# A hybrid attention, gMLP and gated-MLP layer on one core: w_down loaded by quarters, the start of the gate and down stages reordered, part of a norm and of four operand sums on other engines

## The chip, the cores and the metric

The kernel runs on one core of a Trainium2 chip. The metric is the device time of one execution in microseconds (us), the median of several runs. The core has five engines: TensorE (PE in the profile, with PEld for its weight loads), VectorE (DVE), ScalarE (ACT), GpSimd (POOL) and SyncE (SP), whose queue issues nearly all transfers here.

## What is computed

One layer on 1024 tokens of width 1024, cut to what matters here. The first two lines make `x1`; g and up are the gate stage, f the down stage.

```python
mix = concat(diff_attention(...), spatial_gating(...)) @ w_out      # 1024 x 1024
x1  = layer_norm(ALPHA * x + mix, ln1_g, ln1_b)
g   = causal_dwconv(x1 @ w_gate, conv_w, conv_b)                    # 1024 x 2816, width 3
up  = x1 @ w_up                                                     # 1024 x 2816
f   = (silu(g) * up) @ w_down                                       # 2816 x 1024
out = layer_norm(ALPHA * x1 + f, ln2_g, ln2_b)
```

All is float32. Each operand of a large product is split into a high part and a low part (`split`, L214: ScalarE rounds the high part, VectorE or another engine subtracts it from the source for the low part), and `mm3` (L218) makes three matmuls of it: high x high (L220), high x low (L221), low x high (L222).

## The kernel before

The kernel goes through stages: input projections and gMLP, attention (an order written by a list scheduler, L673 to L863), output projection with the first norm (L1061 to L1089), the gate stage (gate and up products with convolution and Silu, up to L1142), the down stage (L1146 to L1254) with the second norm. Outside the attention the tile framework orders the instructions: the program order is the priority, and by an internal estimate of times it moves instructions that are ready ahead of ones that are not, on each engine and on SP's queue too. What runs on an engine or a queue is then a fixed order, and each instruction waits in it for its inputs and for its tile to be free. Pools with `reuse_waits="tile"` may take the place of a released pool and wait only for the tiles that they cover.

**Products of quarters.** Gate, up and down products use a scheme of seven products for a 2 x 2 block product (P1 to P7) in place of eight. `QA` (L904) names the left operand of each (quarters A11, A12, A22 and sums S1 to S4), `QB` (L905) the right one (quarters B11, B21, B22 and sums T1 to T4). In the gate stage the A's are quarters of x1 transposed; a unit u is a pair of 128-column blocks of w_gate (u even) or w_up (u odd), 22 units in all, and one product of a unit is 12 matmuls. In the down stage the A's are quarters and sums of silu(g) * up, which the gate stage writes to DRAM (`yd`, L1045) and the down stage reads back (`ya`); the B's are quarters of w_down, 256 rows to a step m, eleven steps for each product name, in the order P1, P2, P6, P5, P7, P4, P3. A down step is 12 matmuls too (four token tiles by three, `d_mm`).

**From the output projection to the gate stage.** In the loop over t (L1075) each token tile gets its second half, then `lnorm` (L879): statistics, a power on GpSimd, and for each half one subtract-and-scale (L886) and one scale-and-add (L891) on VectorE; with `spread` the latter becomes a scaling on ScalarE (L888) and an addition on GpSimd (L889). `x1_transp(t)` (L914) transposes a tile on TensorE (L925); ScalarE copies and VectorE splits the result, and for tiles 4 to 7 VectorE adds A21 + A22 = S1 (L929). Then `x1_sums` (L936) makes S1's split, S2 = S1 - A11, S3 = A11 - A21 and S4 = A12 - S2, on VectorE (L944), each with a split. In program order come: the transposes of all tiles, S1, two prepared weights, S2, two more, S3, S4 (L1125 to L1135), then the products in the order `seq` (L1097): P1 and P2 of units 0 and 1, then (0, P5), (0, P6), (1, P5), (0, P7), (1, P6), (0, P4), (0, P3), (1, P7). `prepare(n)` (L1118) loads gate weights and makes the first n entries of `order` (T1 of unit 0 first).

**From the gate stage to the down stage.** All 22 blocks of 128 rows of w_down are loaded one after the other (L1148 to L1153), 512 KB each, ten into a new pool `wdp` over the places of the released pools `fp` (gate results) and `qp` (raw gate weights), twelve into tiles `kslot`, which the gate stage uses for prepared weights and S3, S4. Then `d_prep(name, m)` (L1158), kept `DAHEAD` = 4 steps ahead of `d_mm`, loads `ya` and splits both operands; for P6 it also makes T2 by three subtractions on VectorE (L1168 to L1171). Tiles `xslot` (20) hold x1's quarters, S1 and S2 in the gate stage and `ya` and the splits in the down stage.

## Time and profile before

| | |
|---|---|
| time, median of 3 runs | 1119.82 us (1119.18 to 1121.28) |
| profiled execution, its own time | 1121.76 us |
| span of the profiled execution | 1120.1 us |
| PE busy, matmuls | 1069.4 us (95%), 4974 |
| DVE busy | 811.1 us (72%) |
| ACT busy | 476.6 us (43%) |
| POOL busy | 180.7 us (16%) |
| mean granted TensorE clock | 0.982 of full speed |
| DMA | 109.61 MB, 98 GB/s in the mean |

The profile is of one execution. A busy share of an engine says nothing of what waits: that is read from the list of waits, from the timeline of an engine, and from stage tables, which give for a stretch of time (from the span's start) the busy time of each engine and the clock that TensorE was granted, as a share of 2.4 GHz; 0.50 is its lower level, 1.2 GHz. A line number is one of the kernel before; a helper's line (L215, L216 for `split`; L220 to L222 for `mm3`) stands for all of its uses, which the names of the tiles tell apart: `wT`, `wB` are prepared gate weights, `do` and `yo` the split operands of the down stage, `wd` the loaded w_down, `fA` the transposed quarters and their sums, `ps` a PSUM bank.

### The profile page before, as it was taken

Reading aid. Unit: us, or ns where it says so; the run is one execution under the profiler, and the core shown is the slowest. Engines: PE = TensorE matmul, PEld = TensorE weight load, DVE = VectorE, ACT = ScalarE, POOL = GpSimd, SP = SyncE. Lnnn points to the kernel's source line nnn. Section 1 sums busy time; section 2 is a strip of 40 time slices with the busy share of each in tenths; the row PEclk is TensorE's granted clock in tenths of the full one; section 3 lists DMA queues with packets and bytes.
Section 4 is the critical chain, followed back from the end, with each engine's and each line's share of the span. In section 5 each row is a group of like instructions: output and inputs, shape, how many; then the busy total and the mean of one; then the engine's idle time right before and its main releaser. Section 6 shows DMA issues by size and latency. Waiting matters only on the chain.

```text
span 1120.1 us, 13859 instructions
## 1 busy us (share of the span) xinstructions
PE 1069.4 (95%) x4974; PEld 877.7 (78%) x4974; DVE 811.1 (72%) x1349; ACT 476.6 (43%) x894; POOL 180.7 (16%) x209
## 2 busy tenths in 40 slices
PE   9999999888999999899999999999999489999996
PEld 6888887667788887688888888888887368888885
DVE  5337257789998669997677767776876379854777
ACT  5511113348677313565344434443443154444342
POOL 2014044476544011000000000000000000000036
PEclk9999999989999999899999999999999799999999
DMA  7400202111200511032332333133314953423333
GB/s 256 145 10 10 94 27 68 38 38 44 71 11 29 176 49 40 16 132 98 113 123 69 112 112 129 58 113 123 121 39 156 341 198 106 139 87 102 100 98 123
DMA packets 50053, 109.61 MB, mean 98 GB/s; under 512 B 5760, under 2 KB 6288, under 8 KB 49984
## 3 DMA queue, kind: packets, MB, share of 16 engines
q1 hardware_dynamic: 48944, 105.40, 27.8%
q0 software_dynamic: 1040, 3.32, 1.0%
q8 instruction: 39, 0.64, 0.2%
q14 instruction: 30, 0.25, 0.1%
HBM read 82.23 MB, written 24.38 MB: 95 GB/s over the span
## 4 chain that ended last, share of the span: by engine, by line
PE 76%; DVE 13%; DMA 3%; ACT 3%; issue 2%; POOL 2%; SPq 1%; DVEq 0%; POOLq 0%; ACTq 0%
PE ps L222 23%; PE ps L221 23%; PE ps L220 23%; DVE t L438 2%; PE ps L617 2%; DVE p L586 1%; POOL t L441 1%; DVE qs L470 1%; DVE x L886 1%; DMA ya<-yd 1%; PE ps L603 1%; DMA wd<-w_down 1%; PE ps L540 1%; POOL uT L362 1%; DMA zraw<-w_vz 1%
## 5 line engine op out<-in xcount | busy, mean ns | idle before, releaser
L220 PE MATMUL ps<-do,yo 128*128 128x512 f32 x308 | 122.0, 396 | 16.1 <-ACT do L215 16.1
L221 PE MATMUL ps<-do,yo 128*128 128x512 f32 x308 | 122.2, 397 | 0.8 <-DVE do L216 0.8
L222 PE MATMUL ps<-do,yo 128*128 128x512 f32 x308 | 121.5, 394 | 0.0
L216 DVE TENSOR_TENSOR wT<-wq,wT 128x512 fp32r<-128x512 f32 x88 | 60.3, 688 | 34.6 <-ACT wT L215 34.5
L1241 POOL DMA_DIRECT2D g<-ln_g x1 | 0.6, 577 | 520.5 <-DVE do L216 520.5
L216 DVE TENSOR_TENSOR yo<-ya,yo 128x512 fp32r<-128x512 f32 x77 | 54.4, 706 | 39.1 <-ACT yo L215 39.1
L220 PEld LDWEIGHTS ps<-do,yo 128*128 128x128 f32 x308 | 58.9, 191 | 29.8 <-ACT do L215 17.0
L215 ACT ACTIVATE yo<-ya 128x512 fp32r<-128x512 f32 x77 | 48.2, 625 | 76.8 <-DMA ya<-yd 53.7
L215 ACT ACTIVATE wT<-wq 128x512 fp32r<-128x512 f32 x88 | 55.3, 632 | 52.1 <-PE ps L222 46.4
L221 PEld LDWEIGHTS ps<-do,yo 128*128 128x128 f32 x308 | 58.8, 191 | 14.7 <-DVE do L216 2.4
L222 PEld LDWEIGHTS ps<-do,yo 128*128 128x128 f32 x308 | 58.9, 191 | 12.1
L216 DVE TENSOR_TENSOR wB<-wq,wB 128x512 fp32r<-128x512 f32 x66 | 45.5, 690 | 26.8 <-ACT wB L215 24.6
L215 ACT ACTIVATE wB<-wq 128x512 fp32r<-128x512 f32 x66 | 41.3, 631 | 50.2 <-PE ps L222 35.3
L966 DVE TENSOR_TENSOR wq<-wq,wq 128x512 f32<-128x512 f32 x88 | 60.6, 691 | 2.6
L1032 DVE SCALAR_TENSOR_TENSOR c<-g,cw,c 128x1023 f32<-128x1023 f32 (+1 forms) x44 | 56.3, 1279 | 8.0 <-ACT c L1030 7.9
L216 DVE TENSOR_TENSOR do<-wd,do 128x512 fp32r<-128x512 f32 x66 | 45.2, 685 | 19.7 <-ACT do L215 19.7
L215 ACT ACTIVATE do<-wd 128x512 fp32r<-128x512 f32 x66 | 41.0, 621 | 38.2 <-DMA wd<-w_down 19.1
L222 PE MATMUL ps<-xh,qw 128*128 128x512 f32 x128 | 50.9, 398 | 4.2 <-DVE qw L216 4.2
L220 PE MATMUL ps<-xh,qw 128*128 128x512 f32 x128 | 50.9, 397 | 2.2 <-ACT qw L215 2.2
L565 ACT ACTIVATE p<-ps,mx 128x384 f32<-128x384 f32 (+7 forms) x64 | 47.3, 744 | 8.3 <-DVE mx L555 4.4
L221 PE MATMUL ps<-xl,qw 128*128 128x512 f32 x128 | 50.5, 394 | 0.0
L220 PE MATMUL ps<-zw,xh 128*128 128x512 f32 x128 | 49.8, 389 | 0.0
(241 smaller groups left out, 2958.2 us busy)
## 6 DMA issues: line engine op xcount, KB each, us to landing
ya<-yd SPq DMA_DIRECT2D x77, 256.0 KB, 2.9
wq<-w_gate SPq DMA_DIRECT2D x44, 256.0 KB, 2.8
wq<-w_up SPq DMA_DIRECT2D x44, 256.0 KB, 2.8
yd<-u SPq DMA_DIRECT2D x22, 512.0 KB, 3.1
wd<-w_down SPq DMA_DIRECT2D x22, 512.0 KB, 7.3
zraw<-w_vz SPq DMA_DIRECT2D x23, 256.0 KB, 3.1
yd<-c SPq DMA_DIRECT2D x11, 512.0 KB, 2.7
qraw<-w_qk SPq DMA_DIRECT2D x8, 512.0 KB, 3.6
```

Of the source, the lines that this page charges most:

```text
L215: A.activation(hi, src, AF.Copy)
L216: (lo_eng or V).tensor_tensor(lo, src, hi.bitcast(F32), op=ALU.subtract)
L220: PE.matmul(po, lhsT=lh, rhs=rh, start=start, stop=False, skip_group_check=onto)
L221: PE.matmul(po, lhsT=lh, rhs=rl, start=False, stop=False, skip_group_check=onto)
L222: PE.matmul(po, lhsT=ll, rhs=rh, start=False, stop=stop, skip_group_check=onto)
L362: GP.tensor_tensor(u, u, gt.rearrange("p c t -> p (c t)"), op=ALU.mult)
L438: eng.tensor_tensor(t[2][o], pt[i], sin_s[i, cols], op=ALU.mult)
L441: GP.tensor_tensor(t[1], t[1], t[2], op=ALU.add)
L565: A.activation(p[:, 0:L].rearrange("p (b n) -> p b n", b=nb), sc, AF.Exp, bias=st_mx[n][:, j : j + 1], accum_out=sm[:, j : j + 1],)
L617: PE.matmul(st_o[h, i][:, j * DV : (j + 1) * DV], lhsT=st_at[h, i][kt // 4][:, kt % 4, j], rhs=vr[kt // 2][:, kt % 2, h * DV : (h + 1) * D ...
L966: sub = lambda o, a, b: V.tensor_tensor(q[o], q[a], q[b], op=ALU.subtract)
L1032: V.scalar_tensor_tensor(t[:, n:S], g[:, 0 : S - n], cw[:, f, 2 - n : 3 - n], t[:, n:S], op0=ALU.mult, op1=ALU.add)
```

## The change

It does five things.

1. **w_down by quarters.** Each 128 x 1024 block becomes two loads of 128 x 512, issued by `d_loads` just ahead of the product that first needs the quarter: B11 for P1, B21 and B12 for P2, B22 for P6, with `ya` of the same step. Loads run `LAHEAD` = 3 steps ahead of the splits. B11 and B21 of steps 0 to 3 go to tiles of `qp`, which now stays open; the others of steps 0 to 4 to `wdp`, now only over the place of `fp`; the rest to `kslot`.
2. **First down steps in the gate stage.** The loads and splits of P1's steps 0, 1 and 2 are placed behind P2, P6 and P4 of the last unit.
3. **First gate products earlier.** The transposes of tiles 6 and 7 and the sums S1 to S4 are no longer ahead of all products: they follow the first four (`fill_in`). T3 of unit 0 is prepared before S4.
4. **S3 and S4 on GpSimd.** A11 - A21 is taken on GpSimd tile by tile right behind S1's addition, in place; S4's two subtractions go to GpSimd.
5. **The last tile's first norm spread.** For t = 7 `lnorm` uses ScalarE and GpSimd for the second half of its work.

```diff
@@ -31,6 +31,7 @@
 NEG = -1.0e30
 AHEAD = 4
 DAHEAD = 4
+LAHEAD = 3
 SPAN = []
 SCB = 3
 WARM = 10
@@ -926,7 +927,9 @@
             for n in range(2):
                 src = pt[:, 2 * n : 2 * n + 2, :]
                 if name == "A22":
-                    V.tensor_tensor(xf["S1"][n][:, :, tk], xf["A21"][n][:, :, tk], src, op=ALU.add)
+                    f = xf["A21"][n][:, :, tk]
+                    V.tensor_tensor(xf["S1"][n][:, :, tk], f, src, op=ALU.add)
+                    GP.tensor_tensor(f, xf["A11"][n][:, :, tk], f, op=ALU.subtract)
                 else:
                     A.copy(xf[name][n][:, :, tk], src)
                 if name != "A21":
@@ -934,14 +937,13 @@
                     split(hi[:, :, tk], lo[:, :, tk], src)
 
     def x1_sums(name):
-        a, b, slot = {
-            "S1": (None, None, xslot), "S2": ("S1", "A11", xslot), "S3": ("A11", "A21", kslot), "S4": ("A12", "S1", kslot)
-        }[name]
         o = {"S1": "S1", "S2": "S1", "S3": "A21", "S4": "A12"}[name]
-        x_operand(name, slot)
+        x_operand(name, xslot if name in ("S1", "S2") else kslot)
         for n in range(2):
-            if a:
-                V.tensor_tensor(xf[o][n], xf[a][n], xf[b][n], op=ALU.subtract)
+            if name == "S2":
+                V.tensor_tensor(xf[o][n], xf["S1"][n], xf["A11"][n], op=ALU.subtract)
+            elif name == "S4":
+                GP.tensor_tensor(xf[o][n], xf["A12"][n], xf["S1"][n], op=ALU.subtract)
             split(*xo[name][n], xf[o][n])
 
     raws_w, opw, acc_w, dst_w = {}, {}, {}, {}
@@ -1079,7 +1081,7 @@
             e = (n + H) % (2 * H)
             mm_out(pt, t, e, 1, n == 0, n == 2 * H - 1)
         fill_x(t, pt, 1)
-        lnorm(op, x1[t], stats[t], x1[t], g1, b1)
+        lnorm(op, x1[t], stats[t], x1[t], g1, b1, None, t < NT - 1)
         if 2 <= t < 6:
             x1_transp(t - 2)
         if t == 5:
@@ -1122,46 +1124,42 @@
             w_prep(u, name)
             done[0] += 1
 
-    x1_transp(6)
-    x1_transp(7)
-    release(op)
-    fp = tc.alloc_tile_pool(name="fp", bufs=1, reuse_waits="tile")
-    dram = tc.alloc_tile_pool(name="dram", bufs=1, space=bass.MemoryType.DRAM)
-    x1_sums("S1")
-    prepare(2)
-    x1_sums("S2")
-    prepare(4)
-    x1_sums("S3")
-    x1_sums("S4")
-
-
-    for i, (u, name) in enumerate(seq):
-        prepare(max(0, i + AHEAD - 4))
-        product(u, name)
-        outputs(u, name)
-    release(fp)
-    release(qp)
-
-
-    wdp = tc.alloc_tile_pool(name="wdp", bufs=1, reuse_waits="tile")
-    wq = {}
-    for m in range(NM):
-        for kh in range(2):
-            t = wdp.tile([P, D], F32, name=nm("wd")) if m < 5 else kslot([P, D], "wd", F32)
-            f = 2 * m + kh
-            nc.sync.dma_start(t, w_down[f * P : (f + 1) * P, :])
-            wq[m, f"B{kh + 1}1"], wq[m, f"B{kh + 1}2"] = t[:, LEFT], t[:, RIGHT]
-    rows = {}
-    down_seq = [(n, m) for n in ("P1", "P2", "P6", "P5", "P7", "P4", "P3") for m in range(NM)]
+
+    rows, wq, where, wdp = {}, {}, {}, []
+    DORDER = ("P1", "P2", "P6", "P5", "P7", "P4", "P3")
+    down_seq = [(n, m) for n in DORDER for m in range(NM)]
     ya, dop = {}, {}
+    loaded = [0]
+
+    def quarter(m, b):
+
+        if m < 4 and b in ("B11", "B21"):
+            return tslot("dq")
+        if m < 5:
+            return wdp[0].tile([P, 512], F32, name=nm("dq"))
+        key = m, b[1]
+        if key not in where:
+            where[key] = kslot([P, D], "dq", F32)
+        return where[key][:, LEFT if b[2] == "1" else RIGHT]
+
+    def d_load(name, m):
+        a = QA[name]
+        if m % 2 == 0:
+            ya[a, m // 2] = xslot([P, 2, 512], "ya", F32)
+            for i in range(min(2, NM - m)):
+                nc.sync.dma_start(ya[a, m // 2][:, i, :], yd[m + i][:, YI[a], :])
+        for b in {"P1": ("B11",), "P2": ("B21", "B12"), "P6": ("B22",)}.get(name, ()):
+            t = wq[m, b] = quarter(m, b)
+            f, c = 2 * m + int(b[1]) - 1, LEFT if b[2] == "1" else RIGHT
+            nc.sync.dma_start(t, w_down[f * P : (f + 1) * P, c])
+
+    def d_loads(upto):
+        while loaded[0] < min(upto, len(down_seq)) and (wdp or down_seq[loaded[0]][1] < 4):
+            d_load(*down_seq[loaded[0]])
+            loaded[0] += 1
 
     def d_prep(name, m):
         a, b = QA[name], QB[name]
-        if m % 2 == 0:
-            n = min(2, NM - m)
-            ya[a] = xslot([P, 2, 512], "ya", F32)
-            for i in range(n):
-                nc.sync.dma_start(ya[a][:, i, :], yd[m + i][:, YI[a], :])
         sub = lambda o, x_, y_: V.tensor_tensor(o, x_, y_, op=ALU.subtract)
         src = {"T1": "B11", "T3": "B12", "T4": "B21"}.get(b, b)
         if b == "T2":
@@ -1172,16 +1170,41 @@
         elif b == "T3":
             sub(wq[m, "B12"], wq[m, "B22"], wq[m, "B12"])
         ta, tb = xslot([P, 2, 512], "yo"), xslot([P, 2, 512], "do")
-        split(ta[:, 0], ta[:, 1], ya[a][:, m % 2, :])
+        split(ta[:, 0], ta[:, 1], ya[a, m // 2][:, m % 2, :])
         split(tb[:, 0], tb[:, 1], wq[m, src])
         dop[name, m] = ta, tb
 
     ready = [0]
 
     def d_prepare(upto):
+        d_loads(upto + LAHEAD)
         while ready[0] < min(upto, len(down_seq)):
             d_prep(*down_seq[ready[0]])
             ready[0] += 1
+
+    release(op)
+    fp = tc.alloc_tile_pool(name="fp", bufs=1, reuse_waits="tile")
+    dram = tc.alloc_tile_pool(name="dram", bufs=1, space=bass.MemoryType.DRAM)
+    fill_in = [
+        lambda: x1_transp(6), lambda: x1_transp(7), lambda: (x1_sums("S1"), prepare(1)),
+        lambda: (x1_sums("S2"), prepare(4), x1_sums("S3"), prepare(5), x1_sums("S4")),
+    ]
+
+
+    for i, (u, name) in enumerate(seq):
+        prepare(max(0, i + AHEAD - 4))
+        product(u, name)
+        outputs(u, name)
+        if i < len(fill_in):
+            fill_in[i]()
+        if (u, name) == (NU - 1, "P2"):
+            d_prepare(1)
+        if (u, name) == (NU - 1, "P6"):
+            d_prepare(2)
+        if (u, name) == (NU - 1, "P4"):
+            d_prepare(3)
+    release(fp)
+    wdp.append(tc.alloc_tile_pool(name="wdp", bufs=1, reuse_waits="tile"))
 
     dacc = {}
 
@@ -1229,9 +1252,9 @@
         def store(c):
             nc.sync.dma_start(out[t * P : (t + 1) * P, c], r[:, c])
 
-        lnorm(wdp, r, stats2[t], r, rows["g2"], rows["b2"], store, spread)
-
+        lnorm(wdp[0], r, stats2[t], r, rows["g2"], rows["b2"], store, spread)
...
         if name in ("P1", "P2", "P5"):
             for j in range(4):
                 dacc[j, DK.get(name, "a")] = ps1()
@@ -1252,7 +1275,8 @@
                 for m in range(whole, NM):
                     d_mm(name, m, j)
                 d_out(name, j)
-    release(wdp)
+    release(wdp[0])
+    release(qp)
     release(stk)
     for p in reversed(psum):
         p.release()
```

## Rows read from the trace of the kernel before

**Rows 1.** Stage table: from:to, length, busy per engine (instructions), clock, DMA share, GB/s.

```profile
441.00:478.00 37.00, 30.39 (x131) 24.30 (x130) 35.81 (x56) 19.06 (x36) 0.92 (x1) 0.86 0.09 29
478.00:867.00 389.00, 389.00 (x1718) 322.09 (x1717) 292.74 (x412) 173.87 (x259) 0.00 (x0) 1.00 0.30 106
867.00:908.00 41.00, 22.16 (x72) 16.07 (x72) 17.25 (x28) 9.49 (x17) 0.00 (x0) 0.75 0.90 337
908.00:1072.00 164.00, 163.98 (x724) 135.44 (x723) 121.77 (x197) 73.69 (x129) 1.11 (x2) 1.00 0.33 105
```

**Rows 2.** Waits of TensorE, whole run: who <- for whom: us, times, longest.

```profile
PE ps L220 <- ACT do L215: 16.1, 2, 12.7
PE ps L220 <- ACT wT L215: 4.3, 1, 4.3
...
PE ps L925 <- DVE x L891: 2.1, 1, 2.1
PE ps L220 <- ACT u L1007: 1.7, 1, 1.7
...
PE ps L220 <- ACT u L1009: 0.7, 1, 0.7
```

**Rows 3.** Stage table for four stretches right behind waits of TensorE.

```profile
446.60:450.60 4.00, 3.99 (x14) 3.28 (x15) 3.71 (x11) 2.91 (x9) 0.00 (x0) 0.57 0.00 0
472.90:477.80 4.90, 4.78 (x10) 3.30 (x11) 4.84 (x8) 1.58 (x4) 0.00 (x0) 0.50 0.29 93
891.30:897.80 6.50, 6.46 (x15) 4.79 (x16) 5.78 (x9) 1.14 (x2) 0.00 (x0) 0.51 1.02 418
903.60:908.20 4.60, 4.28 (x11) 3.16 (x12) 4.60 (x9) 4.60 (x10) 0.00 (x0) 0.63 0.51 183
```

**Rows 4.** Timeline of TensorE, gate to down stage: start, us, what [idle before].

```profile
878.22 0.39 PE L222 MATMUL ps<-S4h,wB 128*128 128x512 f32 x1
891.34 0.79 PE L220 MATMUL ps<-do,yo 128*128 128x512 f32 x1 [12.73 <-ACT do L215]
```

**Rows 5.** Groups of VectorE, 441 to 474.1 us: count | busy us, mean ns | idle before.

```profile
L944 DVE TENSOR_TENSOR fA<-fA,fA 128x1024 f32<-128x1024 f32 x6 | 7.1, 1217 | 0.0
L216 DVE TENSOR_TENSOR A22l<-ps,A22h 128x256 fp32r<-128x256 f32 x8 | 3.3, 420 | 0.3 <-ACT A22h L215 0.2
L929 DVE TENSOR_TENSOR fA<-fA,ps 128x256 f32<-128x256 f32 x8 | 3.2, 404 | 0.0
L891 DVE SCALAR_TENSOR_TENSOR x<-x,rs,b 128x512 f32<-128x512 f32 x4 | 2.8, 745 | 0.0
...
L216 DVE TENSOR_TENSOR S4l<-fA,S4h 128x1024 fp32r<-128x1024 f32 x2 | 2.4, 1222 | 0.0
```

**Rows 6.** Timeline of VectorE around 474 us.

```profile
473.49 0.68 DVE L216 TENSOR_TENSOR wT<-wq,wT 128x512 fp32r<-128x512 f32 x1
```

**Rows 7.** GpSimd additions: ns min/median/max; group of 128x128 (busy, mean ns).

```profile
L889 POOL TENSOR_TENSOR x<-x,b x14: 1262/1299/1749, 1084.2 to 1112.9; 128x512 f32<-128x512 f32 x14
...
L784 POOL TENSOR_TENSOR obT<-uT,obT 128x128 fp32r<-128x128 f32 x32 | 16.0, 501 | 2.6
```

**Rows 8.** VectorE, norm and down stage, two lines: ns min/median/max.

```profile
L886 DVE SCALAR_TENSOR_TENSOR x<-x,mv,g x32: 736/744/1793, 401.9 to 1114.7; 128x512 f32<-128x512 f32 x32
...
L1200 DVE SCALAR_TENSOR_TENSOR x<-x,ps x16: 627/683/689, 928.5 to 1086.7; 128x512 f32<-128x512 f32 x16
```

**Rows 9.** DMA issues of the page: count, KB each, median us to landing.

```profile
ya<-yd SPq DMA_DIRECT2D x77, 256.0 KB, 2.9
...
wd<-w_down SPq DMA_DIRECT2D x22, 512.0 KB, 7.3
```

**Rows 10.** Timeline of SyncE's queue: start, us from first to last issue, what.

```profile
881.23 10.98 SPq L1152 DMA_DIRECT2D wd<-w_down  x12
```

**Rows 11.** Timeline of ScalarE in the last unit of the gate stage.

```profile
867.60 1.06 ACT L1035 ACTIVATE c<-c 128x1024 f32<-128x1024 f32 x1 [2.14 <-DVE c L1032]
868.56 0.57 ACT L1007 COPY u<-ps 128x512 f32<-128x512 f32 x1
```

2 lines of the change are left out of this document (1 added, 1 removed).

## The prediction, made before the changed kernel was run

> **What bounds the kernel now.** I began with the stage table: in each stretch, how long TensorE (PE) was busy and what clock it was granted. Through the gate stage (478 to 867 us) and most of the down stage PE is busy all the time at full clock, one matmul per 0.226 us (389.00 us for 1718) [rows 1]; there only less PE work would help, and the change leaves the number of matmuls alone. Two stretches are different: 441 to 478 (output projection to gate stage) and 867 to 908 (gate stage to down stage), where PE is busy 30.4 of 37 and 22.2 of 41 us at a mean clock of 0.86 and 0.75 [rows 1]. I call them handover A and B.
>
> Next, the list of who PE waited for. Handover B: 16.1 us for `do`, the split of a piece of w_down, in two waits of 12.7 and 3.4, and 1.7 and 0.7 us for copies of the last unit. Handover A: 4.3 us for `wT`, a prepared gate weight, and 2.1 us for the norm of the last token tile [rows 2]. Behind each wait but the two for copies the granted clock stays low for a while: 4.0 us at 0.57, 4.9 at 0.50, 6.5 at 0.51, 4.6 at 0.63 [rows 3]. The work lost is length times the missing clock: 1.7, 2.45, 3.2 and 1.7 us. So A costs 2.1 + 1.7 + 4.3 + 2.45 = 10.6 us, B 16.1 + 3.2 + 1.7 = 21.0 us. These, and B's 2.4 us for copies, are all that this change can win.
>
> What ends last differs. In B it is transfers: the down stage begins after 22 loads of 512 KB in the order of the rows of w_down, twelve of them issued from 881.2 on, when the last tiles of the gate stage come free [rows 10]; they land after 7.3 us (median), against 2.9 for a load of `ya` [rows 9]; PE's last gate matmul is at 878.2, its first down matmul at 891.3 [rows 4]. In A it is VectorE (DVE), busy 35.8 of 37 us [rows 1], whose order puts the work for S3 and S4 ahead of the weight that PE waits for, which it finishes at 474.2 [rows 6].
>
> **Handover B.** The 22 loads of 512 KB become 44 quarters of 256 KB, the size of `ya`, so I give each 2.9 us [rows 9]; bytes are the same, SP issues 22 more. P1 needs 11 quarters before anything else, not 22 whole rows. The first three steps (two splits each on ScalarE and DVE) move into the last unit of the gate stage, and the quarters of the first four steps go to tiles that held gate weights, which need not wait for the gate stage's end. A step has 12 matmuls, 2.72 us. Three prepared steps and a fourth whose quarter has long landed cover 878.5 + 4 x 2.72 = 889.4. The fifth quarter has its place in the reused gate tiles. At the worst its load is issued at 881.2 as the blocked ones are now, lands after 2.9 to 7.3 us, and its split takes 1.4 (two instructions of 0.68 [rows 6], one after the other): ready at 885.5 to 889.9, late by 0.5 at the worst. From then on a step moves 512 KB (P1) or 768 KB (P2) in 2.72 us, 190 to 290 GB/s; handover B itself moved 337 [rows 1]. The loads run three steps further ahead than before.
>
> What is added to the gate stage: 6 splits on ScalarE and 6 on DVE, 8 us of both together. PE doesn't wait for them, but they stand in the queues among the copies that it does wait for. ScalarE's copy for P6 already comes late, behind a Silu that waits for DVE [rows 11]; one split of 0.63 or a late `ya` in front of it costs PE that much. SP issues these loads ahead of the last stores of `yd`; the down stage needs what those store only in its eleventh step. Cost between 0 and 2 us; I take 1, which also covers the fifth step. B gives 21.0 - 1 = **20.0 us**; bounds 15 (next but one paragraph) and 23.4, if the next stage's matmuls also fill the waits for copies.
>
> **Handover A.** (a) P1 and P2 of the first unit now stand ahead of the transposes of tiles 6 and 7. The 2.1 us wait goes, and with it the 1.7 us of low clock. The last tile's norm gets longer, with its scaling on ScalarE and its addition on GpSimd (POOL), 1.3 us a half [rows 7] instead of 0.7 on DVE [rows 5]; the additions stand on POOL behind S3's subtractions. About 2 to 4 us, covered by two products of 2.72. (b) This alone gives little, as DVE sets the end: it is late for `wT` anyway. Of its chain up to 474.2 the change takes four of six subtractions of line 944 (4.7 us) and two of four instructions of line 891 (1.4), and S4's two lower halves (2.4) now stand behind T3's weight: 8.5 us [rows 5].
>
> (c) What POOL gets: eight subtractions of 128x256, two additions of 128x512, two subtractions of 128x1024. POOL has 0.50 us for 128x128 and 1.26 for 128x512 at the least [rows 7], so I estimate 0.75 and 2.3: 6.0 + 2.5 + 4.6 = 13.1 us. This isn't free for DVE. A DVE instruction with two inputs in SBUF takes 0.74 us alone and up to 1.79 beside POOL's additions, 1.05 lost per addition of 1.29; one that reads PSUM (line 1200) never exceeds 0.69 in the same stretch [rows 7, 8]. So the bounds are 0 and 0.8 x 13.1 = 10.5 us. S3's subtractions fall among 16 DVE instructions that read PSUM (6.5 us [rows 5]) and mostly cost nothing; the 7.1 us of the others meet two-input work: 0.8 x 7.1 = 5.7, less what PSUM readers hide of it. I take 5. The Trainium skill says more (SBUF — State Buffer, "SBUF: two separate sides"): whichever of the two begins first holds the shared pair for its whole instruction and the other waits it out; by that rule DVE would lose all of the 7.1, A would give some 2 us less and the time be 1097. The trace bears it out for the most part: up to 1.05 of 1.29 lost.
>
> DVE's chain to `wT` then ends at 474.2 - 8.5 + 5 = 470.7. PE would be there at 478.3 - 10.6 - 2.7 = 465, so it still waits some 5 us, over P6 and P7. P7 needs this half in its third matmul; the ten that follow take 2.3 us at full and some 4.2 at low clock, so it ends at 473.0 to 474.9 instead of 478.3. A gives **4.5 us**; bounds -2.0 (10.5 blocked, clock low again) and 10.6.
>
> **Sum.** 20.0 + 4.5 = 24.5 us. The profiled execution took 1121.76 us (span 1120.1), 1.9 over the median of the other runs; 1097.3 in its terms is **1095.3** against the median of 1119.82.
>
> **Rivals.** *The port eats A.* DVE loses 10.5 us instead of 5; T3 is ready at 476.2 and A loses 2.0: 1119.8 - 20 + 2 = 1101.8. For it: 1.79 us in the rows; against it: half of POOL's work lies beside PSUM readers. The Trainium skill's rule above points the same way.
>
> *Full cover.* DVE isn't blocked, the order works out, P6 and P7's weights come in time: 10.6 + 21.0 = 31.6, so 1088.2. For it: 8.5 us less to do. Against it: DVE was busy 35.8 of 37 us, so nothing is in reserve.
>
> *It doesn't do what it says in B.* The fifth quarter or a `ya` stands on SP behind a load whose tile isn't free; PE stops once more, as in the second stop now: 3.4 + 1.7 = 5.1 us. B gives 15, the sum 19.5: 1100.3. For it: SP is one queue and issues in order, as with the twelve loads that come only at 881.2 now [rows 10].
>
> *Slower: P6 of the down stage turns DVE-bound.* A step of P6 has three subtractions and two splits on DVE, 5 x 0.68 [rows 6] = 3.4 us against 2.72 of PE. Now the last piece of w_down is asked for by 892.2 [rows 10], and DVE makes these subtractions early; with quarters that come seven steps ahead (4 for the splits, 3 more for the loads) it may come to them late. If PE then stops at each step and its clock stays at 0.50, as behind the waits of [rows 3], eleven steps cost 132 x 0.226 + 11 x 0.7 = 37 us: 1119.8 - 24.5 + 37 = 1132. The point that decides: whether SP issues the B22 quarters before the middle of P2. Against it: their places are free from 881, nothing else holds SP, and P1 and P2 leave DVE half of each step.
>
> **How the numbers follow.** Forecast 0.60, the port 0.15, full cover 0.12, a new stop in B 0.08, P6 slow 0.03, nothing measurable 0.02 (A and B both refilled by later waits). The forecast alone spans 1091 to 1101 (A 2 to 8, B 17 to 21); with port, cover and new stop the range is 1088 to 1103. A measurement here tells 0.2% from no change: faster 0.95, same 0.02, slower 0.03.
>
> **What would show it.** Right: no PE wait for `do` over 1 us and full clock from the last gate matmul on; first down matmul right behind it; no wait for the norm; a wait for `wT` or S2 of some us left in A; DVE two-input instructions of over 1 us beside POOL in A. Wrong: a PE wait within the first six down steps, a clock below 0.9 in P6, or A without any wait.

## The result, and the profile after

The changed kernel takes 1102.9 us (median; 1101.68 to 1103.51), the kernel before 1120.55 us (1119.18 to 1123.05) beside it on the same chip. The ratio is 0.9839, 95% interval 0.9818 to 0.9859: faster, by 17.65 us. Forecast were 1095.3 us and 24.5 us less. The measured time lies outside the 1091 to 1101 that the prediction gave for its forecast alone, and just inside the upper end of its whole range of 1088 to 1103. The profiled execution of the changed kernel took 1102.54 us (span 1100.8, mean granted clock 0.988), the one of before 1121.76 (span 1120.1): 19.2 us between these two. The shares below are of these two executions.

Line numbers have moved by a few (by one up to the first norm, by two in much of the gate stage): `split` is L216 and L217, `mm3` L221 to L223, the norm L887 to L892, S3 on GpSimd L932, S2 and S4 L944 and L946, the loads of `ya` and w_down L1150 and L1154.

The list of PE's waits in the changed kernel (engine, tile and line that waited, who it waited for, us in total, times, longest), of the lines from the gate stage on:

```profile
PE ps L222 <- DVE do L217: 3.3, 3, 1.3
PE ps L221 <- ACT do L216: 2.5, 1, 2.5
...
PE ps L223 <- DVE wT L217: 2.3, 1, 2.3
...
PE ps L221 <- ACT wT L216: 1.7, 1, 1.7
PE ps L221 <- ACT S2h L216: 1.6, 1, 1.6
```

Against [rows 2] the 16.1 us for `do` have shrunk to one wait of 2.5; the waits for the norm (2.1) and for the copies of the last unit (1.7 and 0.7) are gone. In handover A the three last lines and two shorter waits (0.5 and 0.4) make 6.5 us, where the waits of 4.3 and 2.1 made 6.4. A new item is on top: 3.3 us for `do` in three waits, all in the last 30 us.

The stage table of the changed kernel (stretch, its length, then busy time and instructions of PE, PEld, DVE, ACT and POOL, granted clock, DMA share, GB/s):

```profile
441.00:478.00 37.00, 30.56 (x135) 23.58 (x133) 36.24 (x50) 20.11 (x38) 15.27 (x13) 0.91 0.11 33
478.00:867.00 389.00, 389.00 (x1717) 321.97 (x1717) 296.23 (x417) 177.66 (x267) 0.00 (x0) 1.00 0.33 116
867.00:880.00 13.00, 13.00 (x58) 10.55 (x58) 6.94 (x11) 1.45 (x2) 0.00 (x0) 1.00 0.95 317
880.00:884.00 4.00, 4.00 (x20) 3.30 (x19) 0.00 (x0) 0.00 (x0) 0.00 (x0) 1.00 0.95 332
884.00:890.00 6.00, 3.48 (x15) 2.55 (x14) 2.21 (x4) 2.87 (x6) 0.00 (x0) 1.00 1.02 361
...
900.00:1050.00 150.00, 150.00 (x663) 124.23 (x662) 115.84 (x186) 66.82 (x111) 1.12 (x2) 1.00 0.37 115
...
1075.00:1080.00 5.00, 3.04 (x8) 2.18 (x9) 3.65 (x5) 0.00 (x0) 1.72 (x2) 0.76 0.29 108
1080.00:1085.00 5.00, 5.00 (x21) 4.01 (x21) 3.00 (x7) 1.34 (x2) 2.98 (x3) 0.90 0.00 0
```

PE is now full at clock 1.00 from 478 to 884 and from 890 to 1070, but for handover B's 2.5 us. Handover A still has a hole, with DVE busy 36.24 of 37 us, and the last stretch has one that [rows 1] had no reason to look for. The last gate matmul, which the table below counts from, ends at 876.2:

```profile
875.83 0.39 PE L223 MATMUL ps<-S4h,wB 128*128 128x512 f32 x1
```

| where | before | after | gain |
|---|---|---|---|
| last matmul of the output projection ends | 441.80 | 441.24 | 0.6 |
| from there to the last gate matmul, without its waits for copies (2.4) before, without 8 down matmuls (1.8) among them after | 434.4 | 433.2 | 1.2 |
| lost at handover B | 23.4 | 2.5 | 20.9 |
| waits and low clock in the last 45 us | 0.5 | 5.0 | -4.5 |
| from the last matmul to the end of the span | 8.6 | 8.4 | 0.2 |

The table adds up to 18.4 of the 19.2 us between the spans; 0.8 I can't assign. The 5.0 us are 3.3 of waits and, from the last two rows of the stage table, 5 x 0.24 + 5 x 0.10 = 1.7 of low clock.

### The profile page after: what moved, and what is told of

The parts are those of the page before. It is cut to its first block, busy times and chain, and to the rows that moved or that the text cites. A ratio compares the mean times of both kernels' runs of the same rounds, so it can differ in the third digit from the quotient of the medians.

```text
span 1100.8 us, 13950 instructions
## 1 busy us (share of the span) xinstructions
PE 1063.5 (97%) x4974; PEld 873.8 (79%) x4974; DVE 806.4 (73%) x1331; ACT 488.1 (44%) x908; POOL 213.5 (19%) x233
## 4 chain that ended last, share of the span: by engine, by line
PE 78%; DVE 13%; POOL 2%; issue 2%; ACT 2%; DMA 1%; SPq 0%; DVEq 0%; POOLq 0%; ACTq 0%
PE ps L222 24%; PE ps L223 24%; PE ps L221 24%; DVE t L439 2%; PE ps L618 2%; POOL t L442 1%; DVE qs L471 1%; DVE p L587 1%; DVE x L887 1%; PE ps L604 1%; POOL uT L363 1%; PE ps L541 1%; DVE mx L554 1%; PE ps L542 1%; DMA xraw<-xT 1%
## 5 line engine op out<-in xcount | busy, mean ns | idle before, releaser
L222 PE MATMUL ps<-do,yo 128*128 128x512 f32 x308 | 120.9, 393 | 3.3 <-DVE do L217 3.3
L221 PE MATMUL ps<-do,yo 128*128 128x512 f32 x308 | 120.0, 391 | 2.5 <-ACT do L216 2.5
L223 PE MATMUL ps<-do,yo 128*128 128x512 f32 x308 | 120.3, 391 | 0.0
L217 DVE TENSOR_TENSOR wT<-wq,wT 128x512 fp32r<-128x512 f32 x88 | 63.1, 719 | 33.9 <-ACT wT L216 33.9
L216 ACT ACTIVATE wT<-wq 128x512 fp32r<-128x512 f32 x88 | 55.3, 632 | 50.2 <-PE ps L223 43.5
L217 DVE TENSOR_TENSOR yo<-ya,yo 128x512 fp32r<-128x512 f32 x77 | 55.0, 715 | 24.1 <-ACT yo L216 23.8
L221 PEld LDWEIGHTS ps<-do,yo 128*128 128x128 f32 x308 | 58.0, 189 | 15.2 <-ACT do L216 2.9
L216 ACT ACTIVATE yo<-ya 128x512 fp32r<-128x512 f32 x77 | 48.3, 627 | 48.1 <-PE ps L223 46.0
L223 PEld LDWEIGHTS ps<-do,yo 128*128 128x128 f32 x308 | 58.2, 189 | 11.9
L217 DVE TENSOR_TENSOR wB<-wq,wB 128x512 fp32r<-128x512 f32 x66 | 45.9, 698 | 27.0 <-ACT wB L216 20.6
L217 DVE TENSOR_TENSOR do<-dq,do 128x512 fp32r<-128x512 f32 x66 | 47.4, 718 | 22.4 <-ACT do L216 22.4
L216 ACT ACTIVATE wB<-wq 128x512 fp32r<-128x512 f32 x66 | 41.1, 630 | 48.7 <-PE ps L223 33.5
L216 ACT ACTIVATE do<-dq 128x512 fp32r<-128x512 f32 x66 | 41.2, 624 | 46.6 <-DVE yo L217 17.4
L223 PE MATMUL ps<-xh,qw 128*128 128x512 f32 x128 | 51.1, 400 | 4.2 <-DVE qw L217 4.2
L221 PE MATMUL ps<-xh,qw 128*128 128x512 f32 x128 | 50.7, 396 | 2.1 <-ACT qw L216 2.1
L221 PE MATMUL ps<-zw,xh 128*128 128x512 f32 x128 | 49.8, 389 | 0.0
```

The costliest lines, as they stand in the source:

```text
L216: A.activation(hi, src, AF.Copy)
L217: (lo_eng or V).tensor_tensor(lo, src, hi.bitcast(F32), op=ALU.subtract)
L221: PE.matmul(po, lhsT=lh, rhs=rh, start=start, stop=False, skip_group_check=onto)
L222: PE.matmul(po, lhsT=lh, rhs=rl, start=False, stop=False, skip_group_check=onto)
L223: PE.matmul(po, lhsT=ll, rhs=rh, start=False, stop=stop, skip_group_check=onto)
```

## The experiments

All times are medians; the intervals are those of the ratio to the kernel before on the same chip.

| run | us | ratio | 95% interval |
|---|---|---|---|
| the change | 1102.9 | 0.9839 | 0.9818 to 0.9859 |
| e1_down_only | 1104.45 | 0.985 | 0.9835 to 0.9865 |
| e5_gate_only | 1120.96 | 1.000 | 0.9991 to 1.0009 |
| e2_s4_on_vector | 1101.94 | 0.9827 | 0.9812 to 0.9842 |
| e6_order_only | 1106.11 | 0.987 | 0.9856 to 0.9883 |
| e7_norm_on_vector | 1105.72 | 0.9874 | 0.9857 to 0.9892 |
| e10_last_norm_spread | 1105.33 | 0.986 | 0.9838 to 0.9882 |
| e3_fifth_quarter | 1101.15 | 0.9825 | 0.9809 to 0.9841 |
| e4_tail_no_add | 1099.03 | 0.9803 | 0.9788 to 0.9817 |
| e8_norms_behind_splits | 1103.03 | 0.9844 | 0.9829 to 0.9859 |
| e11_tail_on_vector | 1101.7 | 0.9834 | 0.982 to 0.9847 |
| e9_three_mended | 1096.5 | 0.978 | 0.9767 to 0.9794 |
| e12_mended_tail_vector | 1094.72 | 0.9776 | 0.9762 to 0.9789 |

### Each half of the change alone

The down half alone: the gate half of the diff is taken back.

```diff
-                    GP.tensor_tensor(f, xf["A11"][n][:, :, tk], f, op=ALU.subtract)
...
-        lnorm(op, x1[t], stats[t], x1[t], g1, b1, None, t < NT - 1)
+        lnorm(op, x1[t], stats[t], x1[t], g1, b1)
...
+    x1_transp(6)
+    x1_transp(7)
...
-    fill_in = [
-        lambda: x1_transp(6), lambda: x1_transp(7), lambda: (x1_sums("S1"), prepare(1)),
-        lambda: (x1_sums("S2"), prepare(4), x1_sums("S3"), prepare(5), x1_sums("S4")),
-    ]
...
+    x1_sums("S1")
+    prepare(2)
+    x1_sums("S2")
+    prepare(4)
+    x1_sums("S3")
+    x1_sums("S4")
```

> Only the down part of the change: quarters of w_down and the first three down steps in the gate stage; product order, first norm, S3 and S4 as before. Ledger theory (from the trace of after against before: 0.6 us won before 441 us, 1.8 in handover A, 20.4 in handover B, 4.1 lost in the last steps of P3): the 2.4 us of the front are lost again and the rest stays, 1105.3 us, last gate matmul at 878.4 us, PE waits for do of 3 us in the last steps of P3. Rival: the loss in the last steps comes from the shifted gate stage and isn't there: 1101 us.

Measured: 1104.45 us. Handover A waits as before (4.3 for `wT`, 2.1 for the norm); PE waits 2.7 us for the fifth quarter at 889.7, and in the last stretch the same three waits of 0.70, 1.31 and 1.32 us. So the loss at the end comes with the down half, and this half makes nearly the whole gain, 16.6 us against the kernel before on the same chip. Its parts (the smaller loads, the tiles that are free early, the three steps prepared ahead) were not tried one by one.

The gate half alone, on the kernel before: the same lines the other way round.

```diff
-    x1_transp(6)
-    x1_transp(7)
...
-    x1_sums("S3")
-    x1_sums("S4")
+    fill_in = [
+        lambda: x1_transp(6), lambda: x1_transp(7), lambda: (x1_sums("S1"), prepare(1)),
+        lambda: (x1_sums("S2"), prepare(4), x1_sums("S3"), prepare(5), x1_sums("S4")),
+    ]
```

> Only the part of the change that lies at handover A is made on the kernel before (first products ahead of the last transposes, POOL's additions and subtractions); w_down is loaded and prepared as before. Theory 1 (the stretches add up): by the two traces A is worth 1.8 us and the stretch ahead of 441 us 0.6, so 1120.6 - 2.4 = 1118.2; the last gate matmul ends near 876, `do` is still waited for 16 us, and the waits for `do` at the end of the down stage stay at 0.5 us as in the kernel before. Theory 2 (what A gives is passed on, because handover B is set by transfers that begin when the last gate tiles come free, and by nothing earlier): the same 1118. Rival (the forecast of A was right and the whole change took part of it back, by queues that the prepared down steps lengthen): 4.5 us and more, 1116.0 or less, with the last gate mm ending before 874.

Measured: 1120.96 against 1120.92 us, interval of the ratio 0.9991 to 1.0009. The gate half by itself is worth 0 +/- 1 us. The 4.5 us of the forecast are outside that, and so are the 2.4 us that I expected here from the two traces. In its profiled execution the last gate matmul does end 1.7 us earlier than in the kernel before, at 876.9, and PE then waits for `do` as it did (11.42 and 4.47 us). That execution took 1119.27 us, the shortest of eleven, and the one of before 1121.76, well above its median: a difference of 2 us between two single traces is not yet a gain. Nor does handover B swallow a gain there: its two waits are together as long as in the kernel before (15.9 against 16.1 us). With the down half in place the gate half is worth 1.6 us between the medians (1104.45 and 1102.9, timed on different chips; the intervals of their ratios overlap). The two waits in the timeline of PE:

```profile
888.31 0.80 PE L220 MATMUL ps<-do,yo 128*128 128x512 f32 x1 [11.42 <-ACT do L215]
900.63 0.80 PE L220 MATMUL ps<-do,yo 128*128 128x512 f32 x1 [4.47 <-ACT do L215]
```

### Handover A: what GpSimd takes from VectorE

S4's two subtractions back on VectorE.

```diff
             elif name == "S4":
-                GP.tensor_tensor(xf[o][n], xf["A12"][n], xf["S1"][n], op=ALU.subtract)
+                V.tensor_tensor(xf[o][n], xf["A12"][n], xf["S1"][n], op=ALU.subtract)
```

> The changed kernel with the two subtractions of S4 on VectorE again. Port theory (GpSimd's two subtractions hold up VectorE's two-input work): the two S2l instructions take 2.4 us instead of 4.5, the wT split beside them 0.7 instead of 2.8; VectorE loses 2.4 us for its own subtractions and wins 4.3: last gate matmul 2 us earlier, 1101 us. Rival (VectorE has too much work, whoever waits): 2.4 us more work on it, last gate matmul 2.4 us later, 1105 us.

Measured: 1101.94 us. First the timeline of DVE, POOL and PE in the changed kernel (start, duration, what; in brackets the idle time before it and what ended that):

```profile
461.20 2.84 DVE L217 TENSOR_TENSOR wT<-wq,wT 128x512 fp32r<-128x512 f32 x1
463.97 4.52 DVE L217 TENSOR_TENSOR S2l<-fA,S2h 128x1024 fp32r<-128x1024 f32 x2
...
470.69 0.68 DVE L217 TENSOR_TENSOR wT<-wq,wT 128x512 fp32r<-128x512 f32 x1
...
460.23 6.05 POOL L946 TENSOR_TENSOR fA<-fA,fA 128x1024 f32<-128x1024 f32 x2 [4.97 <-DVE fA L944]
...
464.10 0.79 PE L223 MATMUL ps<-S1h,wT 128*128 128x512 f32 x1 [2.31 <-DVE wT L217]
...
476.78 0.50 PE L221 MATMUL ps<-S2h,wT 128*128 128x512 f32 x1 [1.67 <-ACT wT L216]
```

and the same stretch with S4 on VectorE, with the last gate matmul and the wait behind it:

```profile
461.59 0.68 DVE L217 TENSOR_TENSOR wT<-wq,wT 128x512 fp32r<-128x512 f32 x1
462.19 2.35 DVE L217 TENSOR_TENSOR S2l<-fA,S2h 128x1024 fp32r<-128x1024 f32 x2
...
466.73 0.68 DVE L217 TENSOR_TENSOR wT<-wq,wT 128x512 fp32r<-128x512 f32 x1
467.33 2.34 DVE L946 TENSOR_TENSOR fA<-fA,fA 128x1024 f32<-128x1024 f32 x2
...
472.07 0.50 PE L221 MATMUL ps<-S4h,wB 128*128 128x512 f32 x1 [1.92 <-DVE g L1012]
...
872.47 0.39 PE L223 MATMUL ps<-S4h,wB 128*128 128x512 f32 x1
...
884.74 2.08 PE L221 MATMUL ps<-do,yo 128*128 128x512 f32 x4 [2.82 <-ACT do L216]
```

Beside GpSimd's two subtractions (6.05 us) DVE's split of `wT` takes 2.84 instead of 0.68 us and its two splits of S2 4.52 instead of 2.35: 4.3 us lost, for 2.34 us of work handed over. By the Trainium skill (SBUF — State Buffer, "SBUF: two separate sides"), whichever of the two begins first holds their shared ports for its whole instruction, and the other waits until it is done. The trace agrees for the most part: DVE lost 4.3 of GpSimd's 6.05 us. Without GpSimd's subtractions the split of T3's weight begins 4 us earlier (466.73 against 470.69), PE's wait of 2.31 us goes with the low clock behind it (granted clock from 441 to 478 is 1.00 instead of 0.91), and from the output projection to the last gate matmul (down matmuls left out) it takes 429.4 us instead of 433.2. That is more than chance: six traces with the change's own code in this stretch have 433.1 to 434.8. But the total gained only 1.0 us, and the intervals overlap. The wait for the fifth quarter hardly grew: PE stops 9.1 us behind the last gate matmul in both kernels and goes on 11.9 us behind it here, 11.6 in the changed kernel. What took the gain back is low clock: 0.72 from 884 to 890 (1.7 us), and 1.7 us more than in the changed kernel at the end of the down stage. Whether such a wait brings low clock with it, no run here decides (last section).

Of handover A the new order alone: S3 and the first norm back on VectorE too.

```diff
-                    GP.tensor_tensor(f, xf["A11"][n][:, :, tk], f, op=ALU.subtract)
...
+            if name == "S3":
+                V.tensor_tensor(xf[o][n], xf["A11"][n], xf["A21"][n], op=ALU.subtract)
...
-                GP.tensor_tensor(xf[o][n], xf["A12"][n], xf["S1"][n], op=ALU.subtract)
+                V.tensor_tensor(xf[o][n], xf["A12"][n], xf["S1"][n], op=ALU.subtract)
...
-        lnorm(op, x1[t], stats[t], x1[t], g1, b1, None, t < NT - 1)
+        lnorm(op, x1[t], stats[t], x1[t], g1, b1)
```

> The whole change, with S3, S4 and the first norm all on VectorE again, as in the kernel before: of handover A only the new order is left. Theory (beside two-input work POOL takes from VectorE about what it does for it): with S4 alone on VectorE the last gate matmul already ended 3.4 us earlier than in the changed kernel; S3's subtractions and the additions of the first norm are 2.4 and some 10 us of VectorE work, of which only S3 lies in A and behind T3's weight, so the last gate mm ends at 872 to 874 and the time is that of the run with S4 on VectorE, 1101.9, up to 1.5 more for the stretch ahead of 441 us. Rival (POOL is worth its place in all but S4): S3 and the norm on VectorE put 2.4 + 1.4 us back into its chain ahead of S2 and T3, and the time is 1104.5 or more, with a wait for the norm or for wT of over 2 us.

Measured: 1106.11 us, 4.2 more than with S4 alone on VectorE: by the number the rival, though no single wait for the norm or for `wT` is over 2 us (the longest in A is 2.6 us, for `g`). From the output projection's last matmul to the last gate matmul (down matmuls left out) it takes 434.3 us, as long as the kernel before (434.4), and 4.8 more than with S4 alone on VectorE. So the order by itself gives nothing that these traces tell from their scatter. S3 and the norm together are worth their place on GpSimd, and S4 is not; which of the first two it is, this run can't say, and S3 was not tried alone.

The first norm alone back on VectorE:

```diff
-        lnorm(op, x1[t], stats[t], x1[t], g1, b1, None, t < NT - 1)
+        lnorm(op, x1[t], stats[t], x1[t], g1, b1)
```

> The changed kernel with the first norm of tiles 0 to 6 wholly on VectorE again (14 additions of 128x512 leave POOL, 14 scalings leave ScalarE; S3 and S4 stay on POOL). With S3 and this norm both undone the time was 4.2 us longer than with S4 alone undone (1106.1 against 1101.9). Theory (these norms end before handover A, so their engine matters little; S3's subtractions are what counted): 1102 to 1103.5, the last output-projection matmul 0.6 us later, no wait for the norm over 1 us. Rival (VectorE gets out of the output projection with 9.9 us more work, 14 x 0.71, which it does not catch up before T3's weight): the wait for wT is longer than 2.3 us and a wait for the norm of about 2 us stands in A, 1105 or more.

Measured: 1105.72 us, by the number the rival; but what the rival named is not in the trace: no wait for the norm, the same 2.3 us for `wT`, and from the output projection to the last gate matmul 0.4 us more than in the changed kernel, which is within the scatter given above. Of the 1.6 us between the two spans 1.75 are low clock at the end (below). What the norm's place is worth stays open between 0.4 and 2.8 us.

Only the last tile spread, which is what I had taken the change to do:

```diff
-        lnorm(op, x1[t], stats[t], x1[t], g1, b1, None, t < NT - 1)
+        lnorm(op, x1[t], stats[t], x1[t], g1, b1, None, t == NT - 1)
```

> The changed kernel with the first norm of the last tile on three engines and that of tiles 0 to 6 wholly on VectorE: this is what the prediction took the change to do in handover A, while the change does the reverse. Theory (the prediction's cover holds: two products of 2.72 us hide a longer last norm): as with the norm of all tiles on VectorE, 1105 to 1106.5, with no wait for the norm over 1 us and the last gate mm at 876 to 877.5. Rival (the additions of the last tile stand on POOL behind S3's first subtractions, and T3's weight comes later by as much): a wait for the norm over 1 us or a wait for wT of over 3.5 us, the last gate mm after 878.5, 1107.5 or more.

Measured: 1105.33 us, and a wait for the norm of 0.5 us: the theory. One sign is the rival's: the last gate matmul ends at 879.2. But the output projection already ended 1.8 us later in this execution, which took 1107.22 us, the longest of four. The longer last norm is covered by the two products but for the 0.5 us, as the prediction had it.

### Handover B: the fifth quarter

```diff
-        if m < 4 and b in ("B11", "B21"):
+        if b == "B11" and m < 5 or b == "B21" and m < 3:
             return tslot("dq")
...
-        while loaded[0] < min(upto, len(down_seq)) and (wdp or down_seq[loaded[0]][1] < 4):
+        while loaded[0] < min(upto, len(down_seq)) and (wdp or down_seq[loaded[0]][1] < 5):
```

> The changed kernel with B11 of the fifth step in a tile of the gate weights too (B21 of the fourth step gives its place). Theory: the wait of 2.5 us for the fifth quarter goes, as its load no longer waits for the gate results: 1100.4 us, PE without a wait through the first ten down steps. Rival: the sixth quarter or a ya behind it is just as late and PE stops a step later: 1102.9 us.

Measured: 1101.15 us. The medians don't separate it from the changed kernel (its trace also has no low clock at the end, 1.7 us by itself, of which more below); for the quarter the traces do. The timeline of the changed kernel, on SP, ACT and PE:

```profile
878.43 0.32 SPq L1050 DMA_DIRECT2D yd<-u  x1
878.80 5.07 SPq L1154 DMA_DIRECT2D dq<-w_down  x7
...
887.13 0.63 ACT L216 ACTIVATE do<-dq 128x512 fp32r<-128x512 f32 x1 [16.73 <-DMA dq<-w_down]
...
887.81 1.21 PE L221 MATMUL ps<-do,yo 128*128 128x512 f32 x4 [2.52 <-ACT do L216]
```

The quarters behind the gate stage are issued only after the last store of `yd`; the fifth lands at 887.1, and PE has been idle for 2.52 us when its split is done. This hangs on the end of the gate stage: in all nine kernels with this wait, whose last gate matmul ends between 872.9 and 879.2, the first of these loads is issued 2.6 us behind it, PE stops 9.1 us behind it and goes on 10.7 to 11.9 us behind it. With the fifth quarter in a tile that is free ahead of the gate stage's end, the stage table shows PE full there:

```profile
884.00:890.00 6.00, 6.00 (x28) 4.99 (x27) 3.93 (x7) 2.90 (x6) 0.00 (x0) 1.00 0.94 300
```

### The end: norms, splits and GpSimd

The norms of tiles 4 to 7 without their additions on GpSimd (L890), so that these tiles' output lacks b2:

```diff
-                GP.tensor_tensor(o[:, c], o[:, c], b[:, c], op=ALU.add)
+                if add:
+                    GP.tensor_tensor(o[:, c], o[:, c], b[:, c], op=ALU.add)
...
-            finish(4 + j)
+            finish(4 + j, True, False)
```

> The changed kernel without the addition of the second norm's offset for tiles 4 to 7 (left out; their output lacks b2). It frees the port of GpSimd in the last steps of P3 and changes nothing on VectorE's list of work. Port theory: VectorE's splits of 128x512 beside P4's norms take 0.68 us each instead of up to 1.76, PE's waits for do of 3.3 us in all and the low clock behind them go: 1098.5 us. Rival (VectorE has too many instructions ahead of these splits): the waits stay at 2.5 us or more, 1102 us.

Measured: 1099.03 us, 3.9 less than the change. The changed kernel's timeline, DVE, then POOL, then PE:

```profile
1063.66 2.76 DVE L887 SCALAR_TENSOR_TENSOR x<-x,mv,g 128x512 f32<-128x512 f32 x2
...
1066.94 1.70 DVE L217 TENSOR_TENSOR do<-dq,do 128x512 fp32r<-128x512 f32 x1
...
1073.83 1.75 DVE L217 TENSOR_TENSOR do<-dq,do 128x512 fp32r<-128x512 f32 x1
1075.50 1.76 DVE L217 TENSOR_TENSOR yo<-ya,yo 128x512 fp32r<-128x512 f32 x1
...
1066.80 4.68 POOL L890 TENSOR_TENSOR x<-x,b 128x512 f32<-128x512 f32 x3
...
1077.92 0.79 PE L222 MATMUL ps<-do,yo 128*128 128x512 f32 x1 [1.32 <-DVE do L217]
```

and without the additions:

```profile
1066.82 0.67 DVE L217 TENSOR_TENSOR do<-dq,do 128x512 fp32r<-128x512 f32 x1
1067.53 0.63 DVE L217 TENSOR_TENSOR yo<-ya,yo 128x512 fp32r<-128x512 f32 x1
```

A split takes 1.70 to 1.76 us beside an addition and 0.67 without one; two halves of L887 take 2.76 instead of 1.41. Between 1058 and 1078 us DVE loses 7.5 us to eight additions (three pairs of L887 3.4, four splits 4.2). In the kernel before six splits stand behind these norms and the loss is 5.0; in the changed one seven, and PE waits for three of them. The framework that orders the instructions put one more split behind norms that the change doesn't touch. From the first instruction of these norms on DVE to the end it takes 41.0 us in the kernel before, 45.4 in the changed one, and 40.0 without the additions.

The same norms put behind the last splits, with the same work on the same engines:

```diff
-            finish(4 + j)
+            late_norms.append(4 + j)
...
             d_prepare(len(down_seq))
+            for t in late_norms:
+                finish(t)
```

> The changed kernel, but the norms of tiles 4 to 7 are put in the engines' queues behind the last two splits of the down stage instead of ahead of them; work and engines are the same. Theory (the waits at the end are a matter of order: one more split stands behind norms that POOL slows): the three waits for `do` of 0.7, 1.3 and 1.3 us between 1073 and 1078 go, and with them the low clock behind them; 4.1 us less, and 0 to 1.5 of it back as the norms end later: 1098.8 to 1100.3. Rival (the sum of VectorE's and POOL's work in the last 45 us is what sets the end, wherever it stands): the waits go, but the time from the last matmul to the end grows from 8.9 by 3 us or more: 1102 to 1103.

Measured: 1103.03 us: the rival. The three waits go, and PE ends 4.6 us earlier, at 1087.8; but 12.4 us pass from there to the end instead of 8.4. The last instructions of POOL and DVE with the norms behind the splits:

```profile
1092.42 2.48 POOL L890 TENSOR_TENSOR x<-x,b 128x512 f32<-128x512 f32 x2 [0.83 <-ACT x L889]
1094.86 0.55 POOL L885 TENSOR_TENSOR rs<-rs,mhalf 128x1 f32<-128x1 f32 x1
...
1095.45 1.41 DVE L892 SCALAR_TENSOR_TENSOR x<-x,rs,b 128x512 f32<-128x512 f32 x2 [3.60 <-POOL rs L885]
```

and in the changed kernel:

```profile
1094.89 1.00 POOL L885 TENSOR_TENSOR rs<-rs,mhalf 128x1 f32<-128x1 f32 x1
...
1094.20 0.15 DVE L884 TENSOR_SCALAR rs<-mv 128x1 f32<-128x1 f32 x1
...
1096.06 1.40 DVE L892 SCALAR_TENSOR_TENSOR x<-x,rs,b 128x512 f32<-128x512 f32 x2
```

The last tile's power begins at 1094.86 and 1094.89, but not for the same reason. With the late norms POOL's queue sets the end: the chain that ended last runs through POOL's powers and additions and ScalarE's scalings from 1065.9 on, and DVE waits 3.60 us for the last power. In the changed kernel the chain runs from PE's last matmul (1092.4) through DVE; the power's input is there at 1094.35, half a microsecond before POOL is free for it. So two chains end there at nearly the same time, and the run with the late norms frees the one and lengthens the other. What the three waits cost by themselves it doesn't show; it shows that taking them away in this manner is worth nothing.

The same norms in their place, wholly on VectorE:

```diff
-            finish(4 + j)
+            finish(4 + j, False)
```

> The changed kernel with the final norms of tiles 4 to 7 wholly on VectorE, in their old place ahead of the last splits (8 additions leave POOL, 8 scalings leave ScalarE; VectorE gets 8 more instructions of 0.70 us). Theory (in the tail an addition on POOL costs VectorE more than it takes over: in the changed kernel its subtractions and splits between 1058 and 1078 us lose 3.4 + 4.2 = 7.5 us beside 8 additions, against 8 x 0.70 = 5.6 us of own work): VectorE's last split is done about 1.9 us sooner, the waits for `do` between 1073 and 1078 fall from 3.3 to 1.4 us or less, 1099 to 1101. Rival (the additions are better off on POOL): the norms hold VectorE longer, the waits grow, 1103.5 or more.

Measured: 1101.7 us, 1.2 less than the change (the intervals overlap) and 0.7 above the theory's span. All three waits are gone and PE ends at 1088.2; 11.5 us pass from there to the end. From the first norm of these tiles on DVE to the end it takes 43.0 us, against 45.4 in the changed kernel and 43.8 with the norms behind the splits.

### Put together

S4 on VectorE, the fifth quarter early, and the late norms (the diffs of e2, e3 and e8):

```diff
+                V.tensor_tensor(xf[o][n], xf["A12"][n], xf["S1"][n], op=ALU.subtract)
...
+        if b == "B11" and m < 5 or b == "B21" and m < 3:
...
+            late_norms.append(4 + j)
```

> The changed kernel with three edits at once: S4's subtractions on VectorE, the fifth quarter in a tile that is free ahead of the gate stage's end, and the norms of tiles 4 to 7 behind the last splits. Theory (three separate losses that add up): 1102.9 - 1.75 for the quarter, - 3.4 for S4 (which by itself gave only 1.0, since the wait for the quarter grew), - 4.1 for the tail, + 0 to 1.5: 1093.7 to 1095.2, with no wait for `do` over 1 us and a clock of 1.00 from the gate stage to the end. Rival (handover B is set by the transfers, so that what the gate stage ends earlier is waited for there): the last gate mm ends near 872.5, a wait for `do` of 2 to 3 us comes in the first eight down steps, 1097 or more.

Measured: 1096.5 us, with no wait for `do` and full clock from 478 to 1080: above the theory's 1095.2, which fits late norms that give nothing back (e8), and below the rival's 1097. The rival's wait at handover B isn't there. One by one the three edits give 1.0, 1.75 and -0.1 us, together 6.4: behind what S4 gains there is no longer a wait, and no low clock, at handover B or at the end. How much of the rest the late norms give once the stages ahead are mended is open.

The same with the tail of e11 in place of that of e8:

```diff
+                V.tensor_tensor(xf[o][n], xf["A12"][n], xf["S1"][n], op=ALU.subtract)
...
+        if b == "B11" and m < 5 or b == "B21" and m < 3:
...
+            finish(4 + j, False)
```

> The run with three edits (1096.5), but with the norms of tiles 4 to 7 in their old place and wholly on VectorE instead of behind the last splits; S4 on VectorE and the fifth quarter in an early free tile stay. Theory (the time after the last matmul goes back from 12.4 to 8.5 us, since POOL has no work queued there, and of the waits for `do` at the end 0 to 1.4 us with some low clock stay): 1092.5 to 1095.5. Rival (VectorE's work in the last 45 us is what ends last, wherever it stands): 1096 to 1098.

Measured: 1094.72 us, ratio 0.9776 to the kernel before (0.9762 to 0.9789), 8.2 us less than the change and 1.8 less than with the late norms (the intervals of these two ratios overlap). The time is the theory's, but not for its reason: the time behind the last matmul, which the theory had go back to 8.5 us, is 11.6, and no wait for `do` is left. The stage table of this kernel, then the last instructions of POOL and DVE:

```profile
441.00:478.00 37.00, 32.46 (x146) 25.01 (x145) 35.12 (x53) 20.31 (x38) 9.14 (x11) 0.95 0.10 34
...
884.00:890.00 6.00, 6.00 (x29) 4.95 (x28) 5.48 (x9) 2.31 (x4) 0.00 (x0) 1.00 0.95 349
...
1050.00:1070.00 20.00, 20.00 (x89) 16.49 (x88) 20.00 (x39) 4.10 (x7) 3.91 (x4) 1.00 0.31 116
...
1075.00:1080.00 5.00, 5.00 (x23) 4.14 (x23) 4.83 (x10) 1.54 (x3) 4.16 (x4) 1.00 0.27 105
...
1087.11 1.00 POOL L885 TENSOR_TENSOR rs<-rs,mhalf 128x1 f32<-128x1 f32 x1
...
1088.14 1.42 DVE L892 SCALAR_TENSOR_TENSOR x<-x,rs,b 128x512 f32<-128x512 f32 x2 [0.44 <-POOL rs L885]
```

PE is full and at full clock from 478 to its end at 1081.3. DVE is busy for 37.8 of the last 43 us; the chain that ended last runs from 1072.9 on through POOL and ScalarE (powers, scalings and additions of the last four norms) to the last two instructions on DVE, which wait 0.44 us for POOL. What is left to win stands in handover A and in those 11.6 us.

## Why the prediction came out as it did

**What bounds the kernel, and handover B: right.** B gave 20.9 us against 20.0, and the down half alone carries nearly all of the result. PE goes from its last gate matmul into the down stage without a gap, 8 down matmuls already fill the waits for copies, and the transfers move 317 and 332 GB/s there. That the number fits so well has luck in it: the waits for copies gave 2.4 us that the forecast left to its upper bound, and the wait for the fifth quarter took 2.5 where 1 was put down for all costs.

**The fifth quarter: part of its cover was already used.** Transfer and cover both hang on the end of the gate stage, so its earlier end (876.2) changes neither when they are counted from there. The quarter was forecast to be ready 7.0 to 11.4 us behind the last gate matmul, and PE goes on with it 11.6 us behind it: the transfer is just beyond the late end of what was forecast (a quarter lands after 4.5 us in the median, not after 2.9). The cover was put at four steps, 10.9 us, and lasted 9.1: 8 of its 48 matmuls (1.8 us) had gone into the gate stage's waits for copies, where they were a gain. So "late by 0.5 at the worst" became a wait of 2.5 us, 1.8 of it for cover that was already used. The rival "new stop in B" happened, at half its price: 2.5 us instead of 5.1, as the clock stayed at 1.00 behind it. A wait within the first six down steps was also one of the prediction's own signs of being wrong.

**Handover A, part (a): misread.** The condition `t < NT - 1` spreads the norms of tiles 0 to 6, not that of the last tile; item 5 of the change above is wrong in this, and the 1.4 us of line 891 that I took off DVE's chain stayed on it. GpSimd's 14 additions lie between 403 and 443 us. The wait for the norm did go, through the products in front of it; had only the last tile been spread, the products would have covered that too (0.5 us of wait).

**Parts (b) and (c): the chain nearly right, its end not the end of A.** T3's low half was forecast to be ready at 470.7 and is ready at 471.4, P7 ends near 475.1 against 473.0 to 474.9, and PE waits in A as foreseen. That the chain fits has luck in it: the 1.4 us that stayed on DVE were made up elsewhere. The step that failed is the last one, from P7's earlier end to a gain of 4.5 us. PE idles in A as long as before (6.5 us against 6.4), only elsewhere: it begins P7 without a wait (at 472.2), and waits before it for S1, S2 and the weight that is split beside S4's subtractions, and behind it 1.67 us for the next unit's weights, which stand behind S4's halves. Measured gain: 1.2 us between the two traces, 0.8 if the mean of the six above (433.6) is taken, 0 +/- 1 in time where the gate half stands alone.

The price of a 128x1024 subtraction on GpSimd was put too low as well: 3.05 us each against 2.3. DVE lost 4.3 us to these two, and 1.7 us to S3's eight, 6.0 in all where I had 5. S3's subtractions cost little, as I said: beside them DVE's instructions that read PSUM take 0.40 to 0.42 us, as in the kernel before, and only three with two inputs in SBUF are longer. Undoing them and the norm, with S4 on VectorE, lengthens A by 4.8 us. The port rival's mechanism is there, above all for S4, but A gained 1.2 us against the kernel before, where that rival has it lose 2.0. Its time of 1101.8 is close to the result by coincidence.

**The end: the term that is missing in the sum.** I carried everything behind handover B over unchanged. It lost 4.5 us, the largest error. My own [rows 7, 8] came from there: the slow 1.79 us of L886 beside GpSimd's additions are the norms at the end of the kernel. I used them as a price for A and didn't ask how near PE was to waiting for that DVE. In the kernel before it already waited 0.5 us there; one more split behind the norms was enough.

**The sum.** Against the forecast of 24.5 us: -3.3 in A, +0.9 in B, -4.5 at the end, +0.6 ahead of A, +0.2 behind the last matmul make 18.4 of the 19.2 us of the spans. The rest of the way to the measured 17.65 is that the profiled execution of before was 1.2 us above the median beside which the change was timed, and that of the change 0.4 below its own. That 1102.9 lies within the range is luck too: the upper end of 1103 goes back to the port rival, and A did not lose time as that rival has it. What brought the time there is A's smaller gain and the end of the kernel, for which the prediction has no term.

**The rivals that fell.** P6 isn't bound by DVE: PE is full at a clock of 1.00 from 900 to 1050. Full cover didn't come either: it needed the weights of P6 and P7 in time, and handover A free of waits.

## What to carry to other kernels

Count a cover and the transfer that it is to hide from the same event, and leave out of the cover what is used ahead of it: here both moved with the end of the gate stage, and the 8 matmuls that had filled its waits were missing from the cover behind it. Work handed to GpSimd costs where VectorE has two inputs in SBUF: here 4.3 us were lost for 2.3 handed over. Where VectorE read PSUM meanwhile, its instructions didn't get longer (0.40 to 0.42 us beside S3's subtractions). So ask what the other engine will be doing at that minute. When a stage ahead gets faster, look at the last stage too, and judge a wait there by the time of the end: putting the norms behind the splits took three waits of PE away and moved PE by 4.6 us and the end by nothing, as POOL's queue then ended last.
